# A list scheduler's cost model gets measured durations, array mode changes, partition holds and VectorE/GpSimd turns

## The chip, the cores and the metric

The kernel runs as one program on one core of a Trainium2 chip. The metric is device time in microseconds, the median of repeated executions. A profile is one further execution; its own device time was 1646.55 us and its span, from the first to the last recorded instruction, 1644.8 us. Engines are named as the profile names them: PE is TensorE, PEld its weight loads, DVE is VectorE, ACT is ScalarE, POOL is GpSimd and SP is SyncE, on whose queue the DMAs are issued.

## The reference

One layer of a residual block on 1024 tokens of width 1024, all in float32. The input is RMS-normed and projected once (`proj = h @ w_in`); the columns feed two branches and their gates.

```python
# branch 1: stick-breaking attention, 8 heads of 64
z = q @ k.T * Dh**-0.5;  strict = s_idx < t_idx
log_fail = where(strict, log_sigmoid(-z), 0)
after = cumsum(log_fail, reverse=True) - log_fail
o_sb = where(strict, exp(log_sigmoid(z) + after), 0) @ v
# branch 2: RWKV-7 time mixing, 8 heads of 64, one step a token
sa = state @ -kk_t
state = state * w_t + sa (x) (kk_t * a_t) + v_t (x) k_t
y_t = state @ r_t
# merge, output, FFN
merged = gate1 * (o_sb @ w_sb_out) + gate2 * (o_rw @ w_rw_out)
x = x + rms_norm(merged @ w_o)
x = x + rms_norm((silu(h @ w_ffn_gate) * (h @ w_ffn_up)) @ w_ffn_down)
```

## The kernel before, in words

The kernel is written in two layers. The functions `norm_in`, `lora`, `rwkv`, `attention`, `merge`, `output` and `ffn` only record operations (`Block.record`), each with an engine, its operands, a priority (its place in the recording plus an offset) and a cost in nanoseconds (`cost`, line 112). When all is recorded, `Block.issue` runs a list scheduler over the whole program and emits every operation in the order in which the scheduler started it. Each engine then executes its own list strictly in that order, and waits on semaphores where an operand isn't ready. So the costs decide nothing but the order. Because the emitting statement is line 528, every row of the profile and of the order listings carries L528 (L578 in the changed kernel, where the same statement stands lower); rows are told apart by tile names.

The scheduler (`schedule`, `run`, `choose`) keeps, for each engine, the time at which it is free, and for each operation the time at which its inputs are ready: the producer's modelled end plus a hop between the engines (table `LATENCY`) and a margin of 80 ns. It always advances the engine that can start something first, and takes the ready operation of lowest priority number. Tiles get their buffers in the same pass: a buffer is granted when its last user has ended in the model. PSUM has four classes of two buffers each, `d`, `e`, `c` and `y`. The chain of the time mixing has priority (`CHAIN`), gate projections have the lowest (`filler`), and the big projections into `d` fill PE in between.

All large matrix products split each float32 operand into a rounded part and a rest (`split`: an ACT cast, then a DVE subtract) and multiply three times (`mm3`). In the names, `whi` and `wlo` are the two parts of a weight, `big_h` those of the normed input.

The stages, in order of time, with what the prediction speaks of:

- Norm, LoRA and first projections (`norm_in`, `lora`).
- Time mixing (`rwkv`), 4 pairs of heads, two halves of the sequence each. For each half, elementwise work builds the matrices `ar`, `bk`, `nx`; `rw_inverse` inverts triangular 32 by 32 blocks by 31 rows of forward substitution on DVE, each a TENSOR_TENSOR and a TENSOR_REDUCE on tiles `q`, with a trip through DRAM (`nd`, `nl`) ahead and another (`td`) behind; and `rw_chain` carries the state over 8 chunks. One step of it is a matmul of `nx` and the state `sv` into PSUM `c`, copies of its two halves into `xv` by DVE and ACT, a matmul of `bkt` and `xv` into `c`, and two DVE SCALAR_TENSOR_TENSOR into the next `sv`.
- Attention (`attention`, `head`), 4 pairs of heads, 64 blocks of 128 queries in all. A block multiplies queries and keys into PSUM `e` (`kst`, `qst`, `ql`), ACT takes a sigmoid into `nb`, POOL masks the diagonal (AFFINE_SELECT), and DVE runs a multiplying scan over the whole row of 128 to 1024 elements, backwards. PE transposes the result into PSUM `c` four blocks at a time, ACT and DVE split that into two tiles `wt` (the DVE subtract is what gives the `c` buffer back), and PE multiplies them with the split values `vhl` into PSUM `y`. Two operations on `q` and a split into `osb` end a pair of blocks. The projections of the next pair of heads and gate tiles run in between, into `d`.
- Merge, output projection and the FFN (`merge`, `output`, `ffn`), long rows of 512-column matmuls.

The lines that the prediction leans on are the old costs of a matmul into 512 columns, of a transpose and of a DVE operation that is neither a copy, a reduction nor a SCALAR_TENSOR_TENSOR, in `cost` below: `n / 2.4`, `max(out.shape[0], n) / 1.2` and `68 + 1.042 * n`.

## Time and profile before

| | |
|---|---|
| median of 3 executions | 1647.74 us (1647.43 to 1647.74) |
| the profiled execution's own time | 1646.55 us |
| its span | 1644.8 us, granted TensorE clock 0.998 |
| PE busy | 1594.3 us, 97% of the span, 8812 instructions |
| DVE busy | 1121.3 us, 68%, 1999 instructions |
| ACT busy | 717.7 us, 44% |
| POOL busy | 246.8 us, 15% |
| chain of work that ended last | PE 73%, DVE 16%, issue 5% |

A busy PE in this profile is not a PE at its peak: a 512-column matmul is recorded as some 400 ns long, while the next one starts 232 ns after it, so a wait of up to 0.17 us does not show as idle time. A row of a timeline gives the start, the duration, the engine, the operation, the tile written and the tiles read (buffer numbers left out), the shapes and the count; in brackets stands the idle time of the engine just before it and what ended it. In a row of waits stand the total, the number of times and the longest.

### The profile page before, as it was taken

To read this page: it belongs to the slowest core of one execution; us is meant where nothing else is said; L and a number is where in the kernel's file an instruction comes from. 1 tells how busy PE (TensorE), PEld (TensorE's weight loads), DVE (VectorE), ACT (ScalarE), POOL (GpSimd) and SP (SyncE) were. 2 spreads that over 40 slices of the span, in tenths; PEclk is the share of its full clock that TensorE was granted. 3 is DMA by queue.
4 is the path that set the end of the run, shared out by engine and by line. 5 is a ranking of instruction groups with operands and counts; after the bars stand their busy time and mean duration, and the time that the engine had idled before them with its cause. 6 is when DMAs were issued, how large, how long until landed. Compare 5 with 4: busy or idle time off the path is not lost.

```text
span 1644.8 us, 23649 instructions
## 1 busy us (share of the span) xinstructions
PE 1594.3 (97%) x8812; PEld 1272.7 (77%) x8812; DVE 1121.3 (68%) x1999; ACT 717.7 (44%) x1403; POOL 246.8 (15%) x406
## 2 busy tenths in 40 slices
PE   6999999999999999999999999999999999999998
PEld 5777777776777777777787888888888888888886
DVE  6567779668784777778247447766666666777494
ACT  7532334433334756667433434323233223455352
POOL 2021232413214222221014210000000000000000
PEclk9999999999999999999999999999999999999999
DMA  5523222342321000001635411332332322874455
GB/s 217 203 88 92 78 82 80 76 138 65 107 75 37 32 27 14 26 33 52 224 110 182 156 51 52 102 95 92 120 117 100 107 96 96 292 258 147 128 173 179
DMA packets 106963, 180.88 MB, mean 110 GB/s; under 512 B 42336, under 2 KB 43360, under 8 KB 106848
## 3 DMA queue, kind: packets, MB, share of 16 engines
q1 hardware_dynamic: 106848, 179.37, 33.2%
q8 instruction: 69, 1.13, 0.3%
q14 instruction: 46, 0.38, 0.1%
HBM read 129.79 MB, written 47.45 MB: 108 GB/s over the span
## 4 chain that ended last, share of the span: by engine, by line
PE 73%; DVE 16%; issue 5%; ACT 2%; DMA 2%; POOL 1%; SPq 0%; DVEq 0%; POOLq 0%; ACTq 0%
PE d_d L528 31%; PE e_e L528 17%; PE c_c L528 16%; PE y_y L528 10%; DVE q_q L528 6%; DVE b_nb L528 3%; DVE b_wt L528 1%; DVE wlo_wlo L528 1%; DVE b_sv L528 1%; DVE b_nx L528 1%; POOL b_nb L528 1%; ACT b_qst L528 1%; ACT whi_whi L528 0%; DMA b_b<-rows 0%; DVE b_bk L528 0%
## 5 line engine op out<-in xcount | busy, mean ns | idle before, releaser
L528 PE MATMUL d_d<-big_h,whi_whi 128*128 128x512 f32 x1280 | 435.9, 410 | 3.8 <-DVE b_kst L528 2.8
L528 PEld LDWEIGHTS d_d<-big_h,whi_whi 128*128 128x128 f32 x1280 | 235.1, 189 | 52.0 <-issue 6.3
L528 PE MATMUL d_d<-big_h,wlo_wlo 128*128 128x512 f32 x640 | 259.9, 406 | 0.0
L528 PEld LDWEIGHTS d_d<-big_h,wlo_wlo 128*128 128x128 f32 x640 | 121.0, 189 | 24.4 <-issue 1.9
L528 DVE TENSOR_TENSOR wlo_wlo<-raw_raw,whi_whi 128x1024 fp32r<-128x1024 f32 (+1 forms) x60 | 69.4, 1158 | 45.2 <-ACT whi_whi L528 42.0
L528 ACT CAST whi_whi<-raw_raw 128x1024 fp32r<-128x1024 f32 (+1 forms) x60 | 55.9, 933 | 96.8 <-PE d_d L528 85.7
L528 DVE TENSOR_TENSOR q_q<-b_nl,q_q 128x2 f32<-128x2 f32 (+30 forms) x248 | 85.6, 345 | 10.7 <-PE y_y L528 2.7
L528 DVE TENSOR_TENSOR_SCAN b_nb<-b_nb 128x128 f32<-128x128 f32 (+3 forms) x64 | 86.2, 1360 | 9.0 <-POOL b_nb L528 7.7
L528 POOL TENSOR_SCALAR sp_sp<-b_sv,pl_pl 64x64 f32<-64x64 f32 x120 | 57.5, 480 | 117.8 <-DVE b_sv L528 110.8
L528 DVE TENSOR_REDUCE q_q<-q_q 128x1 f32<-128x2 f32 (+30 forms) x248 | 62.0, 250 | 6.7
L528 PE MATMUL d_d<-b_wd,big_act 128*128 128x512 f32 x264 | 66.4, 394 | 0.0
L528 PE MATMUL e_e<-b_wd,big_act 128*128 128x512 f32 x264 | 66.4, 394 | 0.0
L528 ACT CAST b_wd<-b_wraw 128x512 fp32r<-128x512 f32 x71 | 42.1, 620 | 55.5 <-DVE b_wraw L528 22.6
L528 DVE TENSOR_TENSOR b_wd<-b_wraw,b_wd 128x512 fp32r<-128x512 f32 x71 | 46.7, 686 | 22.9 <-ACT b_wd L528 22.8
L528 POOL TENSOR_SCALAR_AFFINE_SELECT b_nb<-b_nb 128x128 f32<-128x128 f32 x64 | 41.2, 653 | 132.1 <-ACT b_nb L528 130.1
L528 PEld LDWEIGHTS e_e<-b_wd,big_act 128*128 128x128 f32 x264 | 49.6, 188 | 11.7
L528 PEld LDWEIGHTS d_d<-b_wd,big_act 128*128 128x128 f32 x264 | 49.6, 188 | 11.6
L528 PE MATMUL c_c<-cst_cst,b_nb 128*128 128x128 f32 x288 | 47.8, 278 | 10.2 <-DVE b_wt L528 6.3
L528 ACT CAST b_wt<-c_c 128x512 fp32r<-128x512 f32 (+2 forms) x96 | 44.1, 480 | 24.5 <-PE c_c L528 23.4
L528 DVE TENSOR_TENSOR b_wt<-c_c,b_wt 128x512 fp32r<-128x512 f32 (+2 forms) x96 | 50.4, 544 | 5.3 <-ACT b_wt L528 4.5
L528 ACT COPY b_xv<-c_c 64x64 f32<-64x64 f32 x64 | 13.3, 207 | 91.9 <-DVE b_xv L528 46.5
L528 PEld LDWEIGHTS c_c<-cst_cst,b_nb 128*128 128x128 f32 x288 | 33.2, 140 | 25.9 <-DVE b_wt L528 12.4
(649 smaller groups left out, 3584.0 us busy)
## 6 DMA issues: line engine op xcount, KB each, us to landing
raw_raw<-w_in SPq DMA_DIRECT2D x42, 512.0 KB, 3.4
raw_raw<-w_fg SPq DMA_DIRECT2D x22, 512.0 KB, 3.5
raw_raw<-w_fu SPq DMA_DIRECT2D x22, 512.0 KB, 4.0
b_wraw<-w_fd SPq DMA_DIRECT2D x22, 512.0 KB, 5.1
act<-b_u SPq DMA_DIRECT2D x40, 256.0 KB, 3.2
b_x<-x SPq DMA_DIRECT2D x16, 512.0 KB, 5.9
b_mg<-gsc SPq DMA_DIRECT2D x28, 256.0 KB, 5.3
raw_araw<-act SPq DMA_DIRECT2D x14, 512.0 KB, 4.4
```

The costliest lines, as they stand in the source:

```text
L528: getattr(getattr(self.real, op.engine), op.method)(**kw)
```

## The change

The costs and the scheduler's state change, and nothing in the recorded program does. `array_mode` gives the part of the PE array that an operation uses, and a change of it adds 90 or 200 ns ahead of the operation in the model, in place of the 3 ns or the load time. A 512-column matmul is costed at 1.5 + 0.4435 n in place of n / 2.4, transposes and full float32 matmuls 2 ns more, a scan at 60 + 2.083 n in place of 68 + 1.042 n, a DVE TENSOR_TENSOR whose first operand has a stride over 16 at 68 + 1.8 n. `held` adds 115 ns on DVE and ACT where the first partition of an operand moves to another group of 32. And a TENSOR_TENSOR or SCALAR_TENSOR_TENSOR with both inputs in SBUF is modelled as waiting for one on the other of DVE and POOL.

```diff
--- before.py
+++ after.py
@@ -109,6 +109,21 @@
     return [(key, p0, p1, f, f + span) for f in starts]
 
 
+def array_mode(op):
+
+    if op.method == "transpose":
+        k, m, whole = op.kw["in_"].shape[0], P, True
+    else:
+        k, m = op.kw["lhsT"].shape[0], count(op.kw["lhsT"].shape[1:])
+        whole = op.kw["lhsT"].dtype == F32R
+    up = lambda x: 32 if x <= 32 else CH if x <= CH else P
+    return up(k), P if whole else up(m)
+
+
+
+INTO_PART, INTO_WHOLE = 90.0, 200.0
+
+
 def cost(engine, method, kw, in_psum):
 
     out = kw.get("out", kw.get("ap"))
@@ -117,11 +132,11 @@
     n = count(out.shape[1:])
     if engine == "tensor":
         if method == "transpose":
-            return max(out.shape[0], n) / 1.2
+            return 2 + max(out.shape[0], n) / 1.2
         m, full = count(kw["lhsT"].shape[1:]), kw["lhsT"].dtype == F32
         if out.shape[0] <= CH and n <= CH:
             return 65.0 if out.shape[0] == CH else 20.0
-        return 2 * max(m, n) / 1.2 if full else max(m / 1.2, n / 2.4)
+        return 2 * (2 + max(m, n) / 1.2) if full else max(m / 2.4, 1.5 + 0.4435 * n)
     psum = any(is_ap(v) and k not in OUTS and in_psum(v) for k, v in kw.items())
     if engine == "vector":
         if method == "tensor_copy" and not psum:
@@ -131,6 +146,10 @@
             return 64 + 1.042 * n
         if method == "scalar_tensor_tensor":
             return max(196, 68 + (1.16 if psum else 1.1) * n)
+        if method == "tensor_tensor_scan":
+            return 60 + 2.083 * n
+        if method == "tensor_tensor" and abs(kw["in0"].ap[-1][0]) > 16:
+            return 68 + 1.8 * n
         return 68 + 1.042 * n
     if engine == "scalar":
         extra = "accum_out" in kw or any(is_ap(kw.get(k)) for k in ("scale", "bias"))
@@ -145,6 +164,12 @@
         return 150 + 2.1 * n
     size = 4 * count(out.shape)
     return max(450.0, size / 360.0)
+
+
+
+
+HELD, HEAD = 115.0, 140.0
+POINTERS = ("scale", "bias", "scalar", "scalar1", "scalar2")
 
 
 class Tile:
@@ -389,6 +414,7 @@
             for q in op.preds:
                 q.succs.append(op)
         free = {e: 0.0 for e in ENGINES}
+        self.begin, self.turn = {}, {}
         waiting = {e: [] for e in ENGINES}
         able = {e: [] for e in ENGINES}
 
@@ -445,14 +471,38 @@
                 at, last = self.run(op, e, at, last, free, done, release, advance)
         return done
 
+    def held(self, op):
+
+
+        reads, writes = self.begin.setdefault(op.engine, ({}, {}))
+        place = lambda ap: (self.in_psum(ap), ap.offset % TSTRIDE // PSTRIDE // 32)
+        ins = [place(v) for k, v in sorted(op.kw.items(), key=lambda x: x[0] in POINTERS) if is_ap(v) and k not in OUTS]
+        outs = [place(v) for k, v in op.kw.items() if is_ap(v) and k in OUTS]
+        held = any(reads.get(m, q) != q for m, q in ins) or any(writes.get(m, q) != q for m, q in outs)
+        reads.update(reversed(ins))
+        writes.update(outs)
+        return held
+
     def run(self, op, e, at, last, free, done, release, advance):
 
+        if e in ("vector", "scalar") and self.held(op):
+            at = max(at, free[e] + HELD)
         if e == "tensor":
             load = count(op.kw["lhsT" if op.method == "matmul" else "in_"].shape[1:]) / 1.2
-            at += max(3.0, load - last.cost if last else 0.0)
+            mode = array_mode(op)
+            if last is not None and mode != array_mode(last):
+                at += INTO_WHOLE if mode == (P, P) else INTO_PART
+            else:
+                at += max(3.0, load - last.cost if last else 0.0)
             last = op
         op.start = at
         op.end = at + op.cost
+        if e in ("vector", "gpsimd") and op.method in ("tensor_tensor", "scalar_tensor_tensor") and not self.in_psum(op.kw["in0"]) and not self.in_psum(op.kw["in1"]):
+
+            other = self.turn.get("gpsimd" if e == "vector" else "vector", 0.0)
+            if other > at:
+                op.end = max(op.end, other + op.cost - HEAD)
+            self.turn[e] = op.end
         free[e] = op.end
         done.append(op)
         for q in op.succs:
```

Counted over the two orders, PE changes its array mode 136 times before and 136 times now. The matmuls, their number and their shapes are the same, and the FFN's rows keep their order.

What moves on DVE is shown at three places. The first is in the attention, at a block with a scan of 896 and one of 1024 elements at the turn from one pair of heads' blocks to the next. SCALAR_TENSOR_TENSOR on `nb` are the scans; TENSOR_TENSOR that read `c` are the subtracts that give a PSUM buffer `c` back. Before:

```order
L528 TENSOR_TENSOR wlo_wlo_6087<-raw_raw_5572,whi_whi_6076 128x1024
L528 SCALAR_TENSOR_TENSOR b_nb_6090<-b_nb_6090 128x896
L528 SCALAR_TENSOR_TENSOR b_nb_6106<-b_nb_6106 128x1024
L528 TENSOR_TENSOR b_vhl_6127<-c_c_6114,b_vhl_6127 128x8x64
L528 TENSOR_TENSOR b_wt_6158<-c_c_6139,b_wt_6152 128x4x128
L528 SCALAR_TENSOR_TENSOR b_nb_6133<-b_nb_6133 128x128
L528 SCALAR_TENSOR_TENSOR b_nb_6137<-b_nb_6137 128x256
L528 TENSOR_TENSOR b_wt_6178<-c_c_6162,b_wt_6171 128x3x128
```

And now:

```order
L578 TENSOR_TENSOR b_osb_902_5670<-q_q_6072,b_osb_901_5657 64x256
L578 SCALAR_TENSOR_TENSOR b_nb_6094<-b_nb_6094 128x896
L578 TENSOR_TENSOR b_vhl_6123<-c_c_6113,b_vhl_6123 128x8x64
L578 SCALAR_TENSOR_TENSOR b_nb_6119<-b_nb_6119 128x1024
L578 TENSOR_TENSOR b_wt_6173<-c_c_6143,b_wt_6157 128x4x128
L578 TENSOR_TENSOR b_wt_6177<-c_c_6155,b_wt_6166 128x3x128
L578 SCALAR_TENSOR_TENSOR b_nb_6133<-b_nb_6133 128x128
```

The split of a weight (`wlo`) has left this place for one further down the list, and the subtract into `vhl` stands in front of the scan of 1024 elements, where it stood behind it.

The second is in the time mixing, at the end of one triangular inverse (the rows on `q` with 128x8 and 128x256) and the start of the next (128x2, 128x1). Before:

```order
L528 TENSOR_TENSOR q_q_3277<-b_nl_3202,q_q_2707 128x256
L528 TENSOR_REDUCE q_q_2707<-q_q_3277 128x8
L528 TENSOR_TENSOR wlo_wlo_3636<-raw_raw_3358,whi_whi_3628 128x1024
L528 STREAM_TRANSPOSE q_q_3676<-q_q_3659 128x256
L528 COPY b_xv_3018<-c_c_3709 64x64
L528 COPY q_q_3730<-y_y_3682 32x256 x2
L528 TENSOR_TENSOR wlo_wlo_3737<-raw_raw_3576,whi_whi_3722 128x1024
L528 TENSOR_TENSOR q_q_3760<-b_nl_3519,q_q_2774 128x2
L528 TENSOR_REDUCE q_q_2774<-q_q_3760 128x1
L528 TENSOR_TENSOR q_q_3760<-b_nl_3519,q_q_2774 128x3
```

And now:

```order
L578 TENSOR_REDUCE q_q_2370<-q_q_3248 128x8
L578 TENSOR_TENSOR q_q_3248<-b_nl_3044,q_q_2370 128x256
L578 TENSOR_REDUCE q_q_2370<-q_q_3248 128x8
L578 TENSOR_TENSOR q_q_3593<-b_nl_3505,q_q_3057 128x2
L578 TENSOR_REDUCE q_q_3057<-q_q_3593 128x1
L578 TENSOR_TENSOR q_q_3593<-b_nl_3505,q_q_3057 128x3
L578 TENSOR_REDUCE q_q_3057<-q_q_3593 128x1
```

The next inverse follows at once; the transpose of the finished one, the copies and two weight splits that stood between them now come later.

The third is in the time mixing too, in the chain of the first half of the second pair of heads: the rows COPY `b_xv` belong to successive steps. Before:

```order
L528 COPY b_xv_1852<-c_c_2815 64x64
L528 SCALAR_TENSOR_TENSOR b_sv_1747<-c_c_2831,pl_pl_902,sp_sp_2813 64x64 x2
L528 COPY b_xv_1852<-c_c_2844 64x64
L528 SCALAR_TENSOR_TENSOR b_tt_2453<-d_d_2788,small_small_202,b_sg_582 128x512
L528 SCALAR_TENSOR_TENSOR b_sv_1747<-c_c_2861,pl_pl_902,sp_sp_2841 64x64 x2
L528 COPY b_xv_1852<-c_c_2892 64x64
L528 SCALAR_TENSOR_TENSOR b_sv_1747<-c_c_2909,pl_pl_902,sp_sp_2890 64x64 x2
L528 STREAM_TRANSPOSE q_q_2920<-q_q_2907 128x256
L528 COPY b_xv_1852<-c_c_2922 64x64
```

And now:

```order
L578 COPY b_xv_1879<-c_c_2736 64x64
L578 TENSOR_REDUCE q_q_2157<-q_q_2620 128x2
L578 TENSOR_TENSOR b_bk_2732<-b_tmp_2018,b_tmp_2502 64x8x64
L578 TENSOR_TENSOR q_q_2620<-b_nl_2404,q_q_2157 128x3x10
L578 TENSOR_TENSOR b_bk_2732<-b_tmp_2018,b_tmp_2502 64x8x64
L578 SCALAR_TENSOR_TENSOR b_sv_1422<-c_c_2751,pl_pl_903,sp_sp_2728 64x64 x2
L578 TENSOR_REDUCE q_q_2157<-q_q_2620 128x3
L578 TENSOR_TENSOR q_q_2620<-b_nl_2404,q_q_2157 128x3x11
L578 TENSOR_REDUCE q_q_2157<-q_q_2620 128x3
L578 TENSOR_TENSOR q_q_2620<-b_nl_2404,q_q_2157 128x3x12
L578 COPY b_xv_1879<-c_c_2774 64x64
```

Rows of an inverse (`q`) and of the elementwise work (`bk`) now stand between the steps of this chain; before, little stood there but the chain itself. Counted over all eight chains, 33 of the 56 pairs of successive steps had a row of an inverse between them before, and 36 have one now.

On PE, in attention blocks 3 to 50 of the 64, between the last matmul of a block's scores and its first transpose there stood 28.3 other PE instructions in the mean, and now 36.1.

## The prediction

> **What bounds the kernel now.** I read the page's engine totals first, then busy times by stretch, then who waited for whom in the stretches with gaps, and last the timelines of DVE and PE at the longest waits.
>
> ```profile
> span 1644.8 us, 23649 instructions
> PE 1594.3 (97%) x8812; PEld 1272.7 (77%) x8812; DVE 1121.3 (68%) x1999; ACT 717.7 (44%) x1403; POOL 246.8 (15%) x406
> ...
> 546.00:768.00 222.00, 207.40 (x1199) 167.88 (x1198) 176.39 (x243) 142.35 (x322) 56.44 (x84) 1.00 0.08 25
> 100.00:546.00 446.00, 432.11 (x3434) 331.20 (x3433) 333.60 (x893) 177.62 (x380) 129.25 (x257) 1.00 0.29 82
> 0.00:100.00 100.00, 85.92 (x382) 69.61 (x383) 55.17 (x66) 61.67 (x112) 15.52 (x41) 1.00 0.53 190
> 768.00:1000.00 232.00, 230.66 (x1052) 187.68 (x1051) 111.78 (x142) 99.89 (x198) 45.58 (x24) 1.00 0.40 136
> 1000.00:1600.00 600.00, 600.00 (x2589) 485.76 (x2588) 421.08 (x617) 224.28 (x359) 0.00 (x0) 1.00 0.40 134
> ```
>
> The columns after the length are PE, PEld, DVE, ACT and POOL busy, then the clock. PE bounds everything. From 1000 to 1600 (the FFN) it never idles: 2589 matmuls in 600 us, 0.232 us each, so an order can win nothing there, nor, with 1.3 us idle, from 768 to 1000. PE waits in the time mixing (100 to 546, 13.9 us idle) and most densely in the attention (546 to 768, 14.6 us idle of 222), where DVE is busy for 79% of the time. Ahead of 100 us PE waits mainly for the first loads, which no order of the engines brings sooner. So the change is worth what it takes from, or adds to, PE's waits between 100 and 768 us.
>
> In the attention nearly all of them are for DVE:
>
> ```profile
> PE c_c L528 <- DVE b_wt L528: 6.3, 11, 1.3
> PE y_y L528 <- DVE b_wt L528: 3.2, 6, 0.8
> PE c_c L528 <- DVE b_vhl L528: 2.2, 3, 0.8
> PE c_c L528 <- DVE b_nb L528: 1.4, 6, 0.4
> ...
> PEld c_c L528 <- DVE b_wt L528: 12.4, 17, 1.7
> PEld y_y L528 <- DVE b_wt L528: 7.7, 13, 1.2
> PEld c_c L528 <- DVE b_vhl L528: 3.6, 3, 1.3
> ```
>
> PE's rows add up to 13.1 us in 26 waits. A matmul is shown some 0.40 us long where the next could start after 0.232, so each wait hides 0.17 us more: 13.1 + 26 x 0.17 = 17.5 us. The weight loads, which wait for the same things, show 23.7 us. I take 17.5.
>
> **The change part by part.** No instruction is added, removed or resized; all that can change is who stands in front of whom.
>
> *Array modes, holds and turns.* With 136 mode changes in both orders, counting them removes none: 0 us. Under the rule that `held` writes down, 350 DVE and 322 ACT operations move to another group of partitions in the old order, 354 and 355 in the new. No view prices that; at the 115 ns that the change assumes, 37 of them are 4.3 us, nearly all on ACT, which is idle 56% of the span: 0 on the path, and at most 4.3 us if none of it were covered.
>
> *The attention, waits behind long scans.* This is the clearest error that the new costs mend.
>
> ```profile
> L528 DVE TENSOR_TENSOR_SCAN b_nb<-b_nb 128x1024 f32<-128x1024 f32 x8 | 18.4, 2304 | 0.4
> ...
> 592.44 4.50 DVE L528 TENSOR_TENSOR_SCAN b_nb<-b_nb 128x896 f32<-128x896 f32 x2 [1.33 <-POOL b_nb L528]
> 596.86 0.66 DVE L528 TENSOR_TENSOR b_vhl<-c_c,b_vhl 128x512 fp32r<-128x512 f32 x1
> ...
> 619.92 2.01 DVE L528 TENSOR_TENSOR_SCAN b_nb<-b_nb 128x896 f32<-128x896 f32 x1
> 621.85 0.44 DVE L528 TENSOR_TENSOR b_osb<-q_q,b_osb 64x256 fp32r<-64x256 f32 x1
> 622.22 2.27 DVE L528 TENSOR_TENSOR_SCAN b_nb<-b_nb 128x1024 f32<-128x1024 f32 x1
> 624.42 0.98 DVE L528 TENSOR_TENSOR b_wt<-c_c,b_wt 128x512 fp32r<-128x512 f32 x2
> ...
> 597.57 0.55 PE L528 MATMUL c_c<-cst_cst,b_nb 128*128 128x128 f32 x3 [0.70 <-DVE b_vhl L528]
> ...
> 625.13 0.55 PE L528 MATMUL c_c<-cst_cst,b_nb 128*128 128x128 f32 x3 [1.30 <-DVE b_wt L528]
> ```
>
> A scan of 1024 elements takes 2304 ns. The old cost makes it 68 + 1.042 x 1024 = 1135 ns, the new one 60 + 2.083 x 1024 = 2193. So the scheduler put two scans of 896 and 1024 in a row and a subtract behind them, and thought PE would get the `c` buffer some 2 us sooner than it does: PE's transposes stood 0.70 and 1.30 us. That happens at three turns between pairs of heads (the `vhl` row: 3 waits, 2.2 us) and, with `wt` behind the scan, at the later blocks of the second and third pair. In the new order the subtract stands in front of the scan of 1024 at all of these five places, 2.3 us sooner, which is more than any of the waits. They go: 2.2 + 3 x 0.17 = 2.7 us and 2 x (1.30 + 0.17) = 2.9 us, together **5.6 us**. What is late next is the scan itself, by the 0.66 us of the subtract; its own transposes have now more PE work ahead of them, the next point.
>
> *The attention, the other waits.* 17.5 - 5.6 = 11.9 us are left, in 21 waits of 0.57 us. Between a block's scores and its transposes PE's list now holds 36.1 instructions in place of 28.3; a PE instruction in this stretch takes 222 / 1199 = 0.185 us, so the cover grows by 1.4 us, above every single wait here. But DVE has the same 176.4 us to do in a shorter stretch, so part of a wait that is covered at one block comes back at the next. Bounds: 0 (all of it comes back) and 11.9 us. Without a row to tell, I take the half: **6.0 us**.
>
> *The time mixing.* Two moves pull against each other. The first shows in DVE's row:
>
> ```profile
> 355.87 0.42 DVE L528 TENSOR_REDUCE q_q<-q_q 128x8 f32<-128x256 f32 x1
> 361.85 1.22 DVE L528 TENSOR_TENSOR wlo_wlo<-raw_raw,whi_whi 128x1024 fp32r<-128x1024 f32 x1 [5.55 <-ACT whi_whi L528]
> 368.24 0.45 DVE L528 STREAM_TRANSPOSE q_q<-q_q 128x256 f32<-128x256 f32 x1 [5.17 <-DMA q_q<-td]
> 371.96 0.22 DVE L528 COPY b_xv<-c_c 64x64 f32<-64x64 f32 x1 [3.27 <-PE c_c L528]
> ...
> 376.06 0.16 DVE L528 TENSOR_TENSOR q_q<-b_nl,q_q 128x2 f32<-128x2 f32 x1 [0.87 <-PE y_y L528]
> ...
> 380.00:405.00 25.00, 23.08 (x179) 16.46 (x179) 23.08 (x71) 7.20 (x19) 9.85 (x19) 1.00 0.19 54
> 488.00:507.00 19.00, 18.57 (x192) 14.94 (x190) 8.23 (x25) 8.77 (x23) 8.41 (x20) 1.00 0.22 54
> ...
> PEld c_c L528 <- DVE b_xv L528: 3.7, 6, 1.2
> ```
>
> Between two inverses DVE waits three times, 14.0 us in all, for a cast, a DRAM trip and a matmul that stand ahead of the ready next inverse; the new list runs that inverse there. The old one runs it from 376 on, under the chain: in 380 to 405 (the last row is that stretch's) PE idles 1.92 us over eight steps, while 488 to 507, seven steps without an inverse on DVE, has 0.43. A step under an inverse thus costs PE 1.92 / 8 - 0.43 / 7 = 0.18 us by its own idle time, and 3.7 / 8 = 0.46 by the weight loads' waits; I take 0.3. The second move is the opposite one: the first chain of the second pair had DVE to itself and now runs under an inverse. Counted over all chains, the step pairs with an inverse between them go from 33 to 36: 3 x 0.3 = **0.9 us lost**. The bounds are 5.0 us won (the chain's whole waits in the next fence: 2.0 + 1.5, and 0.17 for each of the nine) and the loss of the second rival.
>
> ```profile
> PE c_c L528 <- DVE b_xv L528: 2.0, 5, 0.8
> PE c_c L528 <- ACT b_xv L528: 1.5, 4, 0.5
> ...
> PEld c_c L528 <- DVE b_xv L528: 9.4, 18, 1.2
> ```
>
> *The sum.* -5.6 - 6.0 + 0.9 = -10.7 us, on the profiled execution's own 1646.55: 1635.9. That execution lies 1.2 us under the median of the runs shown, 1647.74, so I predict **1637 us**.
>
> **The rivals.** *DVE is the bound of the attention.* Then PE's waits only change place.
>
> ```profile
> DVE q_q L528 <- ACT q_q L528: 14.5, 7, 2.6
> DVE wlo_wlo L528 <- ACT whi_whi L528: 7.8, 7, 1.8
> DVE b_nb L528 <- POOL b_nb L528: 6.1, 4, 2.1
> ...
> L528 POOL TENSOR_SCALAR_AFFINE_SELECT b_nb<-b_nb x60: 287/293/2612, 546.2 to 761.3; 128x128 f32<-128x128 f32 x60
> ...
> 620.55 1.46 POOL L528 TENSOR_SCALAR_AFFINE_SELECT b_nb<-b_nb 128x128 f32<-128x128 f32 x1 [1.57 <-ACT b_nb L528]
> ```
>
> For it: of DVE's 45.6 idle us most are waits for ACT and POOL, and a mask takes 293 ns in the median but up to 2612; the one from 620.55 ends at 622.01, just as the scan from 619.92 does. The new model lets TENSOR_TENSOR and SCALAR_TENSOR_TENSOR take turns with POOL, but not scans, so it still plans these masks too early. Against it: the longest wait, of `q` on ACT, is itself late through PE, whose `y` result ACT reads. If only the 2.7 us at the turns were won and 0.9 lost: 1647.74 - 1.8, **1646 us**.
>
> The Trainium skill, "SBUF — State Buffer", section "Who interferes with whom", says that a DVE instruction with two SBUF inputs locks out a GpSimd instruction that reads SBUF for its whole length. The masks' spread above agrees. By that rule alone the masks would stay behind scans and this rival's 1646 would hold.
>
> *Slower: chain steps behind an inverse.* The first chain of the second pair has now rows of an inverse between all its steps, and more PE work between them doesn't help when DVE itself is behind. Place: these ten step pairs (six in the first half, four more in the second). Price: up to the longest wait of a weight load on `xv`, 1.2 us, each, 12 us. What was relieved elsewhere gives nothing back if those steps waited for something else, and with the attention's 5.6 us alone it comes to 1647.74 + 12 - 5.6 = **1654 us**. It decides once an added wait exceeds some 0.9 us a step with the attention at that lower value. Against it: 0.18 to 0.46 us is what such steps cost before.
>
> *More than forecast.* DVE keeps up, and all 17.5 us of the attention and 5.0 of the chain go: **1625 us**. For it: DVE is at 79% in the attention.
>
> **How the numbers follow.** A measurement of this kernel can't tell less than about 0.2%, 3.3 us, from no change. Forecast 0.55 (its own range 1630 to 1643), more than forecast 0.14, DVE the bound 0.16, slower 0.15. The forecast and the larger gain are faster: with a small part of the middle rival, 0.70; the rest of that rival is the same, 0.15; slower 0.15. The range for 8 in 10 runs from just under the larger gain, 1624, to 1651, within the slower case.
>
> **What would show it.** Right: between 546 and 768 or its counterpart, PE's waits for `vhl` gone and those for `wt` at half; the stretch some 10 us shorter; PE idle in the time mixing within 2 us of 13.9; the FFN's 600 us for 2589 matmuls the same. Wrong: waits of `c` on `nb` in place of those on `wt`, with DVE above 85% (the first rival), or weight loads waiting for `xv` for much more than 9.4 us (the second).

## The result, and where the time came from

The changed kernel takes **1619.51 us** in the median of four executions (1616.39 to 1620.82), against 1647.74. The ratio is 0.9824, with a 95% interval from 0.9807 to 0.9841: 28 us less, where 10.7 were forecast, and 4.5 us below the forecast's range of 1624 to 1651. The profiled execution, which is shown below, took 1620.82 us, 1.3 above its median; its span is 25.8 us shorter than the span before. Its page begins:

```profile
span 1619.0 us, 23662 instructions
...
PE 1583.6 (98%) x8812; PEld 1280.5 (79%) x8812; DVE 1120.1 (69%) x1999; ACT 717.6 (44%) x1403; POOL 249.0 (15%) x406
```

The same engine instructions in nearly the same busy times: PE's is 10.7 us less, and the other engines' differ by at most 8 us. What has gone is mostly waiting.

To compare the stages I cut both spans at the same three places: the first and the last matmul of the chain of the time mixing (`c` from `sv` and `nx`), and the last matmul of the attention (`y` from `wt` and `vhl`). These are busy times by stretch, the kernel before first, with the columns of the prediction (length, then PE, PEld, DVE, ACT and POOL busy with their counts):

```profile
0.00:168.40 168.40, 152.89 (x744) 120.94 (x745) 104.45 (x171) 82.44 (x146) 29.64 (x66) 1.00 0.44 148
168.40:530.10 361.70, 349.25 (x2968) 267.07 (x2967) 275.38 (x772) 146.18 (x325) 112.79 (x227) 1.00 0.29 82
530.10:781.00 250.90, 236.30 (x1381) 191.91 (x1381) 194.49 (x271) 162.20 (x359) 58.79 (x89) 1.00 0.09 31
781.00:1644.80 863.80, 855.90 (x3724) 692.83 (x3722) 546.95 (x786) 326.85 (x575) 45.58 (x24) 1.00 0.40 137
```

And of the changed kernel:

```profile
0.00:174.50 174.50, 156.74 (x763) 124.21 (x764) 108.46 (x175) 83.60 (x149) 28.83 (x68) 0.99 0.42 143
174.50:525.70 351.20, 343.01 (x2962) 270.51 (x2961) 274.23 (x768) 145.63 (x323) 114.61 (x225) 1.00 0.29 85
525.70:756.30 230.60, 230.25 (x1387) 196.36 (x1386) 195.34 (x270) 159.81 (x358) 63.51 (x89) 1.00 0.10 34
756.30:1619.00 862.70, 853.62 (x3707) 689.36 (x3705) 542.05 (x786) 328.59 (x575) 42.09 (x24) 1.00 0.40 137
```

The attention is 20.3 us shorter with 6 PE instructions more, the chain's stretch 10.5 us shorter with 6 fewer, and the rest 1.1 us with 17 fewer. The start is 6.1 us longer; 19 instructions more account for part of that, 2.25 us for more idle time of PE (15.51 before, 17.76 now). The sum is -20.3 - 10.5 - 1.1 + 6.1 = -25.8 us.

The waits tell the same. In the attention PE now waits once, for 0.3 us, where it waited 14.2 us (first fence below, PE's waits in that stretch). Of the weight loads' waits, 23.7 us for `wt` and `vhl` written by DVE have become 1.1, and 16.5 us for `xv` (9.4 for DVE's half, 7.1 for ACT's) have become 3.9 (second fence, PEld's waits over the whole span; the prediction shows all of before but ACT's half, which is the third).

```profile
PE y_y L578 <- ACT b_wt L578: 0.3, 1, 0.3
```

```profile
PEld c_c L578 <- ACT b_xv L578: 2.5, 9, 0.5
...
PEld c_c L578 <- DVE b_xv L578: 1.4, 2, 1.1
...
PEld c_c L578 <- DVE b_wt L578: 0.9, 4, 0.3
...
PEld y_y L578 <- DVE b_wt L578: 0.2, 1, 0.2
```

```profile
PEld c_c L528 <- ACT b_xv L528: 7.1, 13, 1.0
```

Because short waits hide behind a matmul's recorded length, I also use a measure that needs no idle time, and call it **stall**: for each pair of consecutive PE instructions, the time between their starts, less the median of the faster half of all pairs of the same two shapes, summed, with runs of equal small matmuls taken together. It falls from 50.8 to 36.4 us in the chain's stretch, from 36.2 to 14.8 in the attention, and rises from 18.0 to 21.9 at the start and from 9.5 to 12.4 in the rest. Only differences of it are read, since its level depends on how runs of small equal matmuls are counted: taken pair by pair over all 8812 matmuls, it is 85.4 and 71.4 us in the chain's stretch and 34.2 and 15.4 in the attention, and the falls are 14.0 and 18.8 us in place of 14.4 and 21.4.

### The profile page after: what moved, and what is told of

Read it like the earlier page. It is cut to its first block, busy times and chain, and to the rows that moved or that the text cites. A ratio compares the mean times of both kernels' runs of the same rounds, so it can differ in the third digit from the quotient of the medians.

```text
span 1619.0 us, 23662 instructions
## 1 busy us (share of the span) xinstructions
PE 1583.6 (98%) x8812; PEld 1280.5 (79%) x8812; DVE 1120.1 (69%) x1999; ACT 717.6 (44%) x1403; POOL 249.0 (15%) x406
## 4 chain that ended last, share of the span: by engine, by line
PE 86%; DVE 7%; DMA 3%; ACT 2%; issue 1%; POOL 0%; SPq 0%; DVEq 0%; POOLq 0%; ACTq 0%
PE d_d L578 41%; PE e_e L578 19%; PE c_c L578 16%; PE y_y L578 11%; DVE q_q L578 2%; DMA raw_raw<-w_o 1%; DMA b_nl<-nd 1%; DVE b_nx L578 1%; DVE b_bk L578 1%; DMA b_wraw<-w_fd 0%; DMA b_b<-rows 0%; DVE wlo_wlo L578 0%; DVE b_sv L578 0%; DMA b_g<-gsc 0%; DVE b_wraw L578 0%
## 5 line engine op out<-in xcount | busy, mean ns | idle before, releaser
L578 DVE TENSOR_TENSOR q_q<-b_nl,q_q 128x2 f32<-128x2 f32 (+30 forms) x248 | 89.3, 360 | 13.1 <-PE y_y L578 3.8
L578 POOL TENSOR_SCALAR_AFFINE_SELECT b_nb<-b_nb 128x128 f32<-128x128 f32 x64 | 46.0, 728 | 114.4 <-ACT b_nb L578 88.9
L578 PE MATMUL c_c<-b_wd,big_act 128*128 128x512 f32 x198 | 50.9, 395 | 0.3 <-DVE b_wd L578 0.3
L578 ACT CAST b_wt<-c_c 128x512 fp32r<-128x512 f32 (+2 forms) x96 | 43.3, 481 | 16.9 <-PE c_c L578 15.8
L578 PE MATMUL y_y<-b_wd,big_act 128*128 128x512 f32 x198 | 50.6, 394 | 0.0
```

What stands on the lines that cost most here:

```text
L578: getattr(getattr(self.real, op.engine), op.method)(**kw)
```

## The experiments

The theory after the result: two of the new costs bring the gain, each in its own stage. The scan's cost takes the waits out of the attention; the holds (with the strided rows of the inverse, or without) take those out of the chain. The rivals: the true pitch of PE is needed for it, or thousands of places were shuffled and it is chance. The table has all runs. "Attention" and "chain" are the stall in those stretches; the two columns of weight-load waits are those for `wt` and `vhl` written by DVE, and for `xv`; "late copies" are the DVE copies into `xv`, of 64, that start over 0.9 us after the matmul that they read (the earliest start after 0.42).

The kernel before, measured beside each group of versions, took 1648 to 1651 us in the median; differences in the text that are smaller than 10 us go by the ratios.

| version | us | ratio to before, 95% interval | attention | chain | waits `wt`, `vhl` | waits `xv` | late copies |
|---|---|---|---|---|---|---|---|
| before | 1647.7 | | 36.2 | 50.8 | 23.7 | 16.5 | 29 |
| the change | 1619.5 | 0.9824 (0.9807 to 0.9841) | 14.8 | 36.4 | 1.1 | 3.9 | 11 |
| scan alone | 1633.4 | 0.9899 (0.9882 to 0.9915) | 17.6 | 54.3 | 1.8 | 14.5 | 33 |
| without scan | 1644.5 | 0.9967 (0.9954 to 0.9980) | 39.3 | 39.4 | 23.9 | 5.9 | 25 |
| before, margin 84 | 1657.4 | 1.0042 (1.0027 to 1.0057) | 36.7 | 56.5 | 23.7 | 17.6 | 32 |
| PE's costs alone | 1682.6 | 1.0196 (1.0180 to 1.0211) | 41.6 | 64.2 | 22.6 | 18.7 | 36 |
| without holds | 1638.7 | 0.9943 (0.9928 to 0.9958) | 19.6 | 54.4 | 4.6 | 17.8 | 38 |
| without strided rows | 1638.9 | 0.9943 (0.9928 to 0.9959) | 21.3 | 51.8 | 0.7 | 9.5 | 27 |
| without turns | 1625.6 | 0.9862 (0.9841 to 0.9883) | 15.8 | 44.8 | 2.2 | 7.9 | 24 |
| without PE's costs | 1625.4 | 0.9862 (0.9845 to 0.9878) | 23.1 | 43.5 | 4.0 | 3.5 | 12 |
| scan, holds, strided | 1621.0 | 0.9833 (0.9818 to 0.9848) | 13.9 | 45.4 | 0.4 | 2.7 | 15 |
| holds, strided | 1632.3 | 0.9901 (0.9885 to 0.9918) | 27.9 | 45.4 | 19.3 | 2.1 | 12 |
| without modes | 1612.9 | 0.9786 (0.9772 to 0.9801) | 15.0 | 35.8 | 2.9 | 4.3 | 14 |
| the change, margin 84 | 1620.1 | 0.9829 (0.9814 to 0.9843) | 15.6 | 40.5 | 2.9 | 7.8 | 21 |
| holds alone | 1633.3 | 0.9907 (0.9892 to 0.9922) | 32.1 | 40.0 | 20.8 | 5.7 | 15 |
| strided rows alone | 1641.9 | 0.9956 (0.9940 to 0.9973) | 35.4 | 43.1 | 23.6 | 12.5 | 28 |
| without modes, margin 84 | 1618.0 | 0.9814 (0.9799 to 0.9828) | 14.6 | 37.3 | 2.5 | 3.4 | 15 |
| without modes, scans and masks in turns | 1611.1 | 0.9775 (0.9760 to 0.9790) | 13.7 | 32.3 | 0.0 | 4.3 | 14 |
| scan and holds | 1623.2 | 0.9846 (0.9826 to 0.9866) | 16.4 | 43.3 | 0.0 | 4.9 | 14 |
| without modes, scans and masks in turns, margin 84 | 1625.1 | 0.9856 (0.9840 to 0.9873) | 22.7 | 37.4 | 4.1 | 3.6 | 15 |

### The scan's cost, PE's costs and a control

The scan's cost alone, in the kernel before:

```diff
         if method == "scalar_tensor_tensor":
             return max(196, 68 + (1.16 if psum else 1.1) * n)
+        if method == "tensor_tensor_scan":
+            return 60 + 2.083 * n
```

> The kernel before with one new cost alone: a scan at 60 + 2.083 n ns in place of 68 + 1.042 n. Theory S (the attention's gain comes from the scan's true length, through the PE work that the scheduler puts between a block's scores and its transposes): that work grows from 28.3 to 35.2 instructions, about as in the change (36.1), so the waits of c on nb and on wt in the attention nearly go, as they did in the change (10.2 us of idle time of c on nb to 0), and the time falls by about 20 us, to 1625 to 1632. Theory P (the attention's gain needs the true pitch of the 512-column matmul too): within 5 us of 1648. Theory N (any reordering moves the time by some 10 us either way): anywhere from 1637 to 1658, and the control with another margin moves as much.

It gains 1.0%, 17 us, and the stall says where: 36.2 to 17.6 us in the attention, nothing in the chain's stretch. Its weight loads' waits hold both halves of the story, the chain's as before and the attention's gone:

```profile
PEld c_c L564 <- DVE b_xv L564: 8.2, 17, 1.4
...
PEld c_c L564 <- ACT b_xv L564: 6.3, 13, 1.0
...
PEld c_c L564 <- DVE b_wt L564: 1.3, 3, 0.8
```

The mirror of it is the change without those two lines:

```diff
-        if method == "tensor_tensor_scan":
-            return 60 + 2.083 * n
```

> The change with the scan's old cost, everything else new. Theory S: the work between scores and transposes falls back to 26.7 instructions, the waits of c on nb come back, and some 20 us of the 28 are lost: 1635 to 1642; the time mixing keeps its gain. Theory P: within 5 us of the change's 1619.5. Theory N: no reason for any value between 1610 and 1650.

It loses 24 us to the change, somewhat more than expected. The attention's waits are back, the chain's stay low:

```profile
PEld c_c L576 <- DVE b_wt L576: 14.7, 25, 1.1
...
PEld y_y L576 <- DVE b_wt L576: 5.0, 9, 1.3
...
PEld c_c L576 <- DVE b_vhl L576: 4.2, 3, 1.5
PEld c_c L576 <- DVE b_xv L576: 3.3, 7, 1.3
...
PEld c_c L576 <- ACT b_xv L576: 2.6, 8, 0.5
```

Theory S holds for the waits, and nearly for the times, which lie 1.4 and 2.5 us above its ranges. How much of any single time is chance, a control tells:

```diff
-MARGIN = 80
+MARGIN = 84
```

> A control: the kernel before with nothing changed but the margin that the scheduler adds to a hop between engines, 84 ns in place of 80. It reorders thousands of places of the lists without telling the scheduler anything true. Theory S and theory P: within 5 us of 1647.7, since the costs that they name are unchanged. Theory N: off by 8 us or more.

It is 0.42% slower, 6.9 us: more than the 5 that two theories allowed, less than the 8 of the third. So a shuffle with nothing true in it moves a time by some 7 us, and single times that differ by less tell nothing. The waits hardly move (23.7 and 17.6 us), and so are the better witness.

```diff
-            return max(out.shape[0], n) / 1.2
+            return 2 + max(out.shape[0], n) / 1.2
...
-        return 2 * max(m, n) / 1.2 if full else max(m / 1.2, n / 2.4)
+        return 2 * (2 + max(m, n) / 1.2) if full else max(m / 2.4, 1.5 + 0.4435 * n)
```

> The kernel before with the new costs of PE alone (512-column matmul 1.5 + 0.4435 n, transposes and full float32 matmuls 2 ns more, load bound m / 2.4). Theory P: the time mixing and the attention both gain, as PE's modelled list no longer runs ahead of the other engines' lists: 1625 to 1635. Theory S: the attention gains nothing, since the work between scores and transposes is 26.3 instructions, under the old 28.3; what the time mixing gains decides, 1633 to 1648. Theory N: 1637 to 1658.

No theory had this: 32 us slower. The waits for `xv` rise to 18.7 us, the chain's stall to 64.2, the rest's to 18.3. True costs for one engine made the kernel worse. An explanation that fits, but that I only argue: next to a PE that is now slow enough, DVE, whose old costs are too low, looks even more as if it would keep up.

### One part left out at a time

```diff
-        if e in ("vector", "scalar") and self.held(op):
-            at = max(at, free[e] + HELD)
```

> The change without the 115 ns that DVE and ACT lose in the model at a change of partition group. In the change the stretch from the first to the last step of the chain is 10.5 us shorter than before (361.7 to 351.2 us, 2968 and 2962 PE instructions), and the scan alone doesn't bring that. Theory H (the holds do: the copies into xv alternate between the two halves of the partitions, and a chain step is planned 115 ns or more too short without them): the waits of c on xv come back, about 10 us are lost, 1627 to 1633, the attention's 15 us of stall stay. Theory I (the inverse's rows do) and theory T (the turns do): within 7 us of 1619.5, the amount by which the control moved.

19 us are lost, and the waits for `xv` are all back (17.8 us, 38 late copies) while those for `wt` stay away. Theory H by its place; the loss is larger than it said.

```diff
-        if method == "tensor_tensor" and abs(kw["in0"].ap[-1][0]) > 16:
-            return 68 + 1.8 * n
```

> The change without the cost of 68 + 1.8 n for a strided DVE TENSOR_TENSOR (the rows of the inverse; 256 elements take 665 ns, the old cost is 335, the new 529). Theory I: the chain's steps are again planned under inverse rows that last longer than the model thinks; about 10 us are lost in the time mixing, 1627 to 1633. Theories H and T: within 7 us of 1619.5.

The same 19 us, but with half of the waits for `xv` (9.5 us). H and I can't both own 10 us that are the same; the pair had to be taken apart, below.

```diff
-            other = self.turn.get("gpsimd" if e == "vector" else "vector", 0.0)
-            if other > at:
-                op.end = max(op.end, other + op.cost - HEAD)
-            self.turn[e] = op.end
```

> The change without the turns of DVE and POOL. Theory T: about 10 us lost in the time mixing, where POOL works for 114.6 us of 351, so 1627 to 1633. Theories H and I: within 7 us of 1619.5. The attention is unchanged by each of them, since neither scans nor masks take turns in the model.

Some 6 us lost, no more than the control moves: the turns are not shown to bring anything.

```diff
-            return 2 + max(out.shape[0], n) / 1.2
+            return max(out.shape[0], n) / 1.2
...
-        return 2 * (2 + max(m, n) / 1.2) if full else max(m / 2.4, 1.5 + 0.4435 * n)
+        return 2 * max(m, n) / 1.2 if full else max(m / 1.2, n / 2.4)
```

> The change with PE's old costs (512-column matmul n / 2.4, so 213 ns where the next one starts after 232). Alone, the new PE costs made the kernel 32 us slower. Theory A (the parts add up): this one is about 32 us faster than the change, near 1590. Theory B (PE's true pitch pays only once the other engines' costs are true too: a model in which PE alone is slow believes that DVE keeps up): the gain of the whole is partly PE's, 1620 to 1640, though the work between scores and transposes grows to 69.5 instructions and the attention's stall stays at 15 us or falls.

Some 6 us lost. Theory A, by which the parts add up, falls by 35 us. B's time is right, but the attention's stall rose to 23.1 and didn't stay at 15: with 69.5 instructions between scores and transposes, so more such work is not always less waiting.

### Which parts are enough

```diff
+        if method == "tensor_tensor_scan":
+            return 60 + 2.083 * n
+        if method == "tensor_tensor" and abs(kw["in0"].ap[-1][0]) > 16:
+            return 68 + 1.8 * n
...
+        if e in ("vector", "scalar") and self.held(op):
+            at = max(at, free[e] + HELD)
```

> The kernel before with three of the new parts only: the scan's cost, the holds at a change of partitions and the strided rows; PE's costs, the array modes and the turns stay old. Theory D (the true costs of DVE and ACT are the whole gain, and PE's, the modes and the turns are within the chance of a reordering): within 8 us of the change, 1612 to 1627. Theory E (PE's costs and modes are needed for it, or the turns are): above 1630.

1621.0 us: these three bring as much as the whole change, to within chance. The same without the scan's lines:

```diff
-        if method == "tensor_tensor_scan":
-            return 60 + 2.083 * n
```

> As the last, without the scan's cost: the holds and the strided rows alone. Theory D: the time mixing gains (stall from the first to the last chain step from 51 us to 40 or less), the attention gains nothing (its stall stays at 36 us or more, since only the scan's cost moved it in the runs so far): 1633 to 1641. Rival L (what counts in the attention is the length of the work between scores and transposes, whatever made it long; it is 44.8 instructions here, against 28.3 before and 36.1 in the change): the attention's stall falls to 20 us or less as well, and the time is 1615 to 1627.

16 us gained, 0.7 under the range of theory D; rival L falls, since the waits for `wt` and `vhl` stay at 19.3 us with 44.8 instructions of cover. Theory D is not clean either: the attention's stall did fall, to 27.9 where it said 36 or more, and the chain's fell only to 45.4 where it said 40 or less, though the waits for `xv` are down to 2.1 us.

```diff
-            if last is not None and mode != array_mode(last):
-                at += INTO_WHOLE if mode == (P, P) else INTO_PART
-            else:
-                at += max(3.0, load - last.cost if last else 0.0)
+            at += max(3.0, load - last.cost if last else 0.0)
```

> The change without the 90 and 200 ns for a change of the array's mode. My forecast gave this part 0. Theory D: within 8 us of 1619.5, 1612 to 1628. Theory E: above 1630.

6.3 us faster than the change. The control at this end, in the change:

```diff
-MARGIN = 80
+MARGIN = 84
```

> A control at the other end: the change with a margin of 84 ns in place of 80 and nothing else. What it moves is chance of the reordering, and bounds what the runs that leave out one part can tell. Expected within 8 us of 1619.5, as the same control moved the kernel before by 6.8; if it goes as far as 1635 or more, the losses of the runs without holds and without strided rows (19 us each) can't be told from chance.

It moves by 0.8 us. Not every shuffle costs something, then; the 19 us of the two runs above look like more than one, the 6 of turns and PE's costs do not. A later control, below, moves by 13 us, so that the times alone leave less room than this one suggests.

### The pair taken apart

The holds alone, in the kernel before:

```diff
+        if e in ("vector", "scalar") and self.held(op):
+            at = max(at, free[e] + HELD)
```

> The kernel before with the holds alone. Without the holds the change is 19 us slower, without the strided rows as well, and the two together without the scan's cost bring 16 us. Theory J (they work only as a pair: a chain step runs beside inverse rows, and its end comes out right only when both lengths are): within 7 us of 1648, and the weight loads' waits for xv (16.5 us before, 2.1 with the pair) stay above 10 us. Theory K (each is worth some 8 us by itself): 1636 to 1643, those waits near 9 us.

They alone bring 15 us, all that the pair brings, and take the waits for `xv` from 16.5 to 5.7: theory J falls. Theory K, which gave them half of that, is missed by 2.7 us.

```profile
PEld c_c L564 <- DVE b_wt L564: 10.3, 15, 2.1
...
PEld y_y L564 <- DVE b_wt L564: 8.1, 14, 1.1
...
PEld c_c L564 <- ACT b_xv L564: 2.9, 6, 0.8
PEld c_c L564 <- DVE b_xv L564: 2.8, 7, 0.9
```

The strided rows alone, in the kernel before:

```diff
+        if method == "tensor_tensor" and abs(kw["in0"].ap[-1][0]) > 16:
+            return 68 + 1.8 * n
```

> The kernel before with the strided rows' cost alone. Theory J: within 7 us of 1648, waits for xv above 10 us. Theory K: 1636 to 1643, those waits near 9 us. The work between scores and transposes happens to be 42.7 instructions here, as in the run with both, so if the length of that work alone counts, part of the attention's waits go (stall from 36 to about 28 us) and 8 us come from there.

7 us, as much as chance, with 28 late copies and 12.5 us of waits for `xv`. The attention's stall stays at 35.4 with 42.7 instructions of cover, so the length of the cover alone doesn't count. The holds carry most of the chain's gain. Whether that stands with the scan's cost beside it, one more run asks:

```diff
+        if method == "tensor_tensor_scan":
+            return 60 + 2.083 * n
...
+        if e in ("vector", "scalar") and self.held(op):
+            at = max(at, free[e] + HELD)
```

> The kernel before with the scan's cost and the holds only. Alone, the scan's cost brought 17 us, the holds 15, the strided rows 7, which the control with another margin moves too. Theory F (two errors, two stages, and the strided rows by chance): the gains add up, 17 + 15 = 32, less what the starts and ends lose: 1616 to 1624, and the DVE copy into xv starts at most 0.75 us after its matmul in the median (0.86 before, 0.71 with the holds alone). Theory G (the strided rows are needed beside the holds, as the change without them says, 1638.9): 1630 or more, with a copy that starts 0.8 us or later.

1623.2 us, a median copy 0.68 us after its matmul, 14 late copies and 4.9 us of waits: theory F. The two costs together are the change, to within chance, without strided rows, PE's costs, modes and turns. Why the change without its strided rows is 16 us slower than this version stays open; a bad order by chance would do it, but isn't shown.

### The modes and the masks

The change without modes, with the other margin:

```diff
-MARGIN = 80
+MARGIN = 84
```

> The change without the array modes, which was 6.6 us faster than the change, with a margin of 84 ns besides. If leaving out the modes is a true gain, it holds under another shuffle of the lists: 1608 to 1617. If it was chance, 1617 to 1627 is as likely.

1618.0 us: the gain of leaving out the modes was mostly chance. Then my first rival's masks, in the version without modes:

```diff
-        if e in ("vector", "gpsimd") and op.method in ("tensor_tensor", "scalar_tensor_tensor") and not self.in_psum(op.kw["in0"]) and not self.in_psum(op.kw["in1"]):
+        both = op.method in ("tensor_tensor", "scalar_tensor_tensor") and not self.in_psum(op.kw["in0"]) and not self.in_psum(op.kw["in1"])
+        if e in ("vector", "gpsimd") and (both or op.method in ("tensor_tensor_scan", "affine_select")):
```

> The change without the array modes, and with scans on DVE and masks on POOL also taking turns in the model, which the change leaves out. A mask takes 653 ns in the mean before and 728 in the change, against 293 by itself. My first rival said that these masks bound the attention. If that is so in the new order, the attention's stall (15 us) falls by 5 us or more: 1605 to 1609. If the longer work between scores and transposes already covers them: within 4 us of 1613.

1611.1 us, within 4 of 1613: nothing more to win there. The interval of this version's ratio lies below the change's, so it is the fastest order of all that ran, but not by what its costs say, since with the other margin it loses 13 us, to 1.1 us above the range that a lucky shuffle was given:

```diff
-MARGIN = 80
+MARGIN = 84
```

> The fastest version so far (no array modes, scans and masks in the turns) with a margin of 84 ns: if its 1611 is more than a lucky shuffle, it stays under 1616; if not, it goes to 1616 to 1624, as the version without the modes did.

**What the runs say together.** The four versions with neither the scan's cost nor the holds took 1642 to 1683 us, the five with one of them 1632 to 1645, the eleven with both 1611 to 1639. The waits separate without overlap: for `wt` and `vhl` 0 to 4.6 us in all thirteen versions with the scan's cost, 19.3 to 23.9 in the seven without; for `xv` 2.1 to 9.5 in the fourteen with holds, 12.5 to 18.7 in the six without. Since a shuffle moved a time by up to 13 us, the waits are better evidence than any single time.

The strided rows are not shown to be chance. In all four pairs of versions that differ by them alone, the waits for `xv` are lower with them (16.5 without and 12.5 with, then 5.7 and 2.1, 4.9 and 2.7, 9.5 and 3.9 us), and the times too, by 7, 1, 2 and 19 us. The chain's stall is lower in two of the pairs and higher in two. A small true part of the gain fits this; how large it is stays open, and so does what the 115 ns on DVE and those on ACT bring apart, since each run has both or neither.

## Why the prediction was wrong, step by step

**What bounds the kernel** was right: PE, nothing to win after the attention (1.1 us there), everything between 100 and 768 us. That the start has nothing to give held; it got 2.25 us worse.

**The attention: right mechanism, too small.** The forecast was 5.6 + 6.0 = 11.6 us, the stretch is 20.3 shorter. At a turn between pairs of heads, as the one that I quoted, the subtract into `vhl` now stands ahead of the scan of 1024 elements (timeline of DVE in the changed kernel, then that of PE at the same place):

```profile
641.33 2.02 DVE L578 TENSOR_TENSOR_SCAN b_nb<-b_nb 128x896 f32<-128x896 f32 x1 [0.19 <-POOL b_nb L578]
643.27 0.67 DVE L578 TENSOR_TENSOR b_vhl<-c_c,b_vhl 128x512 fp32r<-128x512 f32 x1
643.85 2.28 DVE L578 TENSOR_TENSOR_SCAN b_nb<-b_nb 128x1024 f32<-128x1024 f32 x1
```

```profile
644.15 0.40 PE L578 MATMUL d_d<-big_h,whi_whi 128*128 128x512 f32 x1
644.39 0.93 PE L578 MATMUL c_c<-cst_cst,b_nb 128*128 128x128 f32 x7
```

It ends at 643.94 and the transposes start at 644.39, without a wait. Two choices made the forecast small. "I take the half" of the other waits: all went, and none came back at the next block. And "I take 17.5" as the sum of all waits: the weight loads' 23.7 us stood beside it. Of the 20.3 us, PE's idle time shows 14.3 (14.6 before, 0.35 now), and the idle time of PEld falls by 24.8 (250.90 - 191.91 = 59.0 before, 34.2 now). Adding 0.17 us to each *visible* wait leaves out those that are shorter than 0.17 and so not visible at all.

**The holds at 0: the step that failed.** The sum had them at 0 us, and at most at a loss of 4.3; alone they brought 15 us. I wrote that no view prices them. The timeline does. The end of one row and the start of the next show whether DVE overlapped two instructions; here is the chain's copy on DVE in the kernel before and, behind it, in the change:

```profile
392.12 0.75 DVE L528 TENSOR_TENSOR b_bk<-b_r,b_tmp 64x512 f32<-64x512 f32 x1
392.91 0.27 DVE L528 TENSOR_REDUCE q_q<-q_q 128x5 f32<-128x105 f32 x1
393.20 0.22 DVE L528 COPY b_xv<-c_c 64x64 f32<-64x64 f32 x1
393.34 0.37 DVE L528 TENSOR_TENSOR q_q<-b_nl,q_q 128x132 f32<-128x132 f32 x1
```

```profile
347.78 0.30 DVE L578 TENSOR_REDUCE q_q<-q_q 128x6 f32<-128x144 f32 x1
348.12 0.22 DVE L578 COPY b_xv<-c_c 64x64 f32<-64x64 f32 x1
348.26 0.42 DVE L578 TENSOR_TENSOR q_q<-b_nl,q_q 128x150 f32<-128x150 f32 x1
```

In both the reduce has ended when the copy starts (in the change at 348.08, the copy at 348.12), while the row behind the copy starts 0.08 ahead of the copy's end (348.26 against 348.34). Over the kernel before, an instruction that `held` names starts 32 ns after the end of the one ahead of it in the median (350 of them), any other 73 ns before that end (1648). None of the 350 starts before that end, and 55% of the others do. The medians are 105 ns apart, so the old plan lacked up to 350 x 0.105 = 37 us of DVE, an estimate; 76 of the 350 waited over 0.1 us and may have lost nothing by it. The Trainium skill, "VectorE: DVE Perf Modes", section "Two Vector instructions with no wait between them", has the rule: an instruction that starts in another group of 32 partitions is held until all earlier ones have finished. The records agree with it, and give it this price. Where ACT is concerned, the records look alike: none of the 322 starts before the end of the one ahead of it, and 48% of the others do.

I asked what the cost removes on the chip, where it removes nothing, and not what it does to the plan. A plan that knows when DVE comes free also knows when the copy will start. The start times that the scheduler itself plans show the error: for the 64 copies of the kernel before it planned 0.50 us from matmul to copy in the median, with 6 over 0.9 us, where the chip took 0.85, with 29. `held` names 51 of these copies. With the holds alone the plan says 0.61 and the chip 0.71. In the mean over the copies the chip is 0.28 us later than the plan before, 0.09 with the holds alone, 0.26 with the strided rows alone, 0.06 in the change, 0.33 in the change without the holds and 0.22 in the change without the strided rows. In the place shown above, the old plan had 0.64 us, and `held` names all three rows from 392.12 to 393.20.

PE's timeline shows what it costs. Before, with the copy at 393.20, 1.34 us after the matmul that it reads, four matmuls don't fill the step:

```profile
391.86 0.46 PE L528 MATMUL c_c<-b_sv,b_nx 128*128 128x128 f32 x2
392.08 0.71 PE L528 MATMUL d_d<-big_h,whi_whi 128*128 128x512 f32 x2
392.62 0.39 PE L528 MATMUL d_d<-big_h,wlo_wlo 128*128 128x512 f32 x1
392.86 0.40 PE L528 MATMUL d_d<-big_h,whi_whi 128*128 128x512 f32 x1
393.48 0.38 PE L528 MATMUL c_c<-b_xv,b_bkt 128*128 128x128 f32 x1 [0.22 <-DVE b_xv L528]
```

In the change, with the copy at 348.12, 0.64 us after its matmul, four do:

```profile
347.48 0.42 PE L578 MATMUL c_c<-b_sv,b_nx 128*128 128x128 f32 x2
347.66 0.47 PE L578 MATMUL d_d<-big_h,whi_whi 128*128 128x512 f32 x1
347.98 0.39 PE L578 MATMUL d_d<-big_h,wlo_wlo 128*128 128x512 f32 x1
348.21 0.62 PE L578 MATMUL d_d<-big_h,whi_whi 128*128 128x512 f32 x2
348.67 0.45 PE L578 MATMUL c_c<-b_xv,b_bkt 128*128 128x128 f32 x2
```

**The time mixing: wrong sign.** I counted the steps that run beside an inverse and gave each the same price, 0.3 us, for +0.9 us; the stretch is 10.5 us shorter, and PE's idle time in it fell from 12.5 to 8.2 us, by more than the 2 us that I allowed. That count missed what decides, namely whether the copy comes in time *within* such a step. Of 64 copies by DVE, 29 started over 0.9 us after their matmul, now 11. Of the 14.4 us of stall that this stretch lost, 6.2 lie at the matmuls on `xv` (8.2 to 2.0) and 2.2 at those of `q` and `nx` (3.0 to 0.8); 6.8 lie at `d` matmuls (20.8 to 14.0), and I could trace these to nothing. Taken pair by pair, these three are 8.3, 2.2 and 3.7 us.

**The rivals.** DVE as the bound of the attention: it is now busy for 195.34 / 230.60 = 85% of it, and PE waits once. The masks are still late, even later (groups on POOL, before and then in the change):

```profile
L528 POOL TENSOR_SCALAR_AFFINE_SELECT b_nb<-b_nb 128x128 f32<-128x128 f32 x64 | 41.2, 653 | 132.1 <-ACT b_nb L528 130.1 <-DVE b_osb L528 1.3 <-DVE b_nb L528 0.6
```

```profile
L578 POOL TENSOR_SCALAR_AFFINE_SELECT b_nb<-b_nb 128x128 f32<-128x128 f32 x64 | 46.0, 728 | 114.4 <-ACT b_nb L578 88.9
```

728 ns in the mean where it was 653: the mechanism is there, and yet PE no longer waits for it. That the longer cover, 36.1 instructions, hides it fits the run with masks in the turns, which gained no more than chance, but isn't shown apart from it. Chain steps behind an inverse: the waits for `xv` fell, though 36 pairs of steps have inverse rows between them in place of 33: this rival is refuted. More than forecast was the one that came, 5.5 us past its 1625: it took the attention at 17.5 us and the chain at 5.0.

## What to carry to other kernels

When a change makes a plan's costs true, ask what the plan does differently once it knows them, not what the hardware then does differently: a cost that removes no instruction and no stall by itself was worth about half of this gain (15 of 28 us). Take the wait time that there is to win from the engine that shows it (here the weight loads), not from one whose records overlap, and look for short waits in start-to-start times. And before a scheduler's parts are credited one by one, change something that means nothing: here a margin of 4 ns moved the time by 1 to 13 us.

## What was not expected of the hardware

A hold at a change of partitions is visible in the records, as 105 ns between a start 32 ns after the last end and one 73 ns before it. And, of the plan rather than of the hardware: PE's true costs alone made the kernel 32 us slower, while leaving them out of the change cost some 6 us, within what a shuffle does.
